# Attention heads in couples: score products alternate between the halves of TensorE's rows, value products between the halves of its columns

## The chip, the cores and the metric

The kernel runs on one core of a Trainium2 chip, in one launch. The metric is the time of an execution on the device in microseconds (us). Three runs of the kernel before took 1774.15, 1775.56 and 1777.96 us. The core's engines work side by side and each takes its own instructions in its own order: TensorE (PE, with PEld for the loads of its weights), VectorE (DVE), ScalarE (ACT), GpSimd (POOL), and SyncE (SP), which here issues the loads of the weights.

## The reference

Two blocks of two layers each on x [1, 256, 1024] in float32; the output of the first is the input of the second. What matters here are the products with only 64 rows or 64 columns:

```
first block, per layer:
  xn = rms_norm(h); proj = xn @ w_in                      # queries, keys, values, gates, RWKV inputs
  y_a: 8 query heads of 64 on 2 key heads, mask = the 64 best causal keys of an indexer
       s = q k^T / 8 ; p = softmax(s + mask) ; o = p v
  y_b: a short convolution, gated
  y_c: RWKV-7, 8 heads of 64: zw = w0 + tanh(lw) @ w_up ; a = sigmoid(a0 + la @ a_up)   # 64 rows each
       a recurrence over the tokens, here in chunks of 64 tokens by products of [64, 128] with [64, 128]
  h += (sum of the gated branches) @ w_out ; h += conv_glu_ffn(rms_norm(h))
second block, per layer:
  a: 16 heads of 64, a mixture of dilated causal patterns, here one softmax with one additive table
  b: 8 differential heads: softmax(q1 k1^T) - lambda softmax(q2 k2^T), each of 64 rows, times v [256, 128]
  h += (sigmoid(ga) (ya @ w_proj_a) + sigmoid(gb) (yb @ w_proj_b)) @ w_out
```

## The kernel before

Features lie on the 128 partitions, tokens along the free dimension. All large products with weights are made three times in float32r, from weights and activations split into a high and a low part (lines 206 to 208 and 244 to 246); ACT makes the high parts (line 184), DVE the low ones (line 185), SP's queue brings the raw weights. All small products are float32, and each such matmul shows in the trace as two passes. I call the products with the weights the stream.

A head of 64 features uses half of the array. Its scores (`softmax`, line 436) are two matmuls at line 445 with 64 rows, on the upper or the lower half of the rows as the head is even or odd: 128 queries by 128 keys, then 128 by 256. DVE adds the mask and takes the extreme (line 447), ACT takes the exponential and the sums (450), DVE the reciprocal (452) and, or ACT in the first block (458), the scaling. `flip_probs` transposes the probabilities in three PE instructions (481) and ACT copies them out (483). `apply` makes the head's output with two matmuls (489 and 490) of 64 columns, written to the upper or lower half of a PSUM bank's partitions. Scores and flips take their banks from the pool `at`, which has two; the outputs take one bank of `pv`.

`pipelined` emits for step i the scores of head i, the probabilities of head i - 1 and the output of head i - 2, with a third of a step between the three. In the second block's part b one step has two softmaxes, of both halves of a differential head. In the first block eight heads make a layer's attention; in the second, two groups of eight heads (part a) and two of four differential heads (part b) make a layer. `rw_prepare` makes the two low-rank products (line 764) one after the other, four matmuls each on one half of the rows. `rw_scores` makes for each of four chunks four matmuls (850) on the upper half of the rows and then four on the lower, each four into one bank of the pool `rk` (two banks). The second block does not use `rk`.

The order of the engines' work comes from two places. `interleave` merges the streams (RWKV, attention and the bulk of projections in the first block; bulk and attention in the second) by estimated times, of which the table `TUNE` gives the factors. Then a scheduling layer below the kernel orders each engine's instructions by readiness, so that a stage's matmuls can be parted by instructions of the stream; the rows under "The change" show what it made of it.

Of the kernel before, what the change touches and what calls it, by code (L numbers as in the profile page):

```python
# [17 lines left out]
S = 256  # L18
# [13 lines left out]
def _const_table():  # L32
    """Tables that depend on the shapes alone, one row per partition."""
# [45 lines left out]
# y <- (x y^2 + RSQRT[0]) y, then with a = x y^2: ((c2 a + c1) a + c0) y  # L79
# [26 lines left out]
def interleave_gen(a, b):  # L106
    """two streams in turn"""
    live = [a, b]
    while live:
        for g in list(live):  # L110
            try:
                yield next(g)
            except StopIteration:
                live.remove(g)


class Core:
# [25 lines left out]
    def slot(self, *shape, dt=F32, name="s", extra=False):  # L143
        """a tile of up to 4 KB per partition from the shared slots, or from those of the present phase"""
# [44 lines left out]
    # ---- activations as matmul operands: pairs of 128-row k tiles (hi, lo), feature on the partition  # L189
# [11 lines left out]
    def block(self, ps, hi, lo, x, ks, nk):  # L201
        """k tiles ks (of nk) of one block of 128 output features [128, 256]"""
# [7 lines left out]
    def feature_pair(self, src, c0, x, nk, pool=None, between=(), ready=None):  # L210
        """two blocks of 128 output features side by side in one bank: [128, 2, 256]; between: calls to make after each"""
# [61 lines left out]
    def rstd(self, ss, n, eps):  # L273
        """(ss / n + eps) ** -0.5 in place"""
# [39 lines left out]
    def squares(self, c, src=None, out=None, ts=(0, 1)):  # L314
        """sums of squares of half c of the columns"""
# [8 lines left out]
    def raw_half(self, g, c, squares=True):  # L324
        """after half c of h is there: its part of the operand without the norm's scale, and of the scale"""
# [16 lines left out]
    def norm_scale(self, eps, ss=None, ts=slice(0, 2)):  # L342
        """the norm's scale of every token [128, 2]"""
# [6 lines left out]
    def rows_of(self, r):  # L350
        """r [128 tokens, 2] along the free dimension of every partition [128, 256]"""
# [10 lines left out]
    def normalise(self, rb, x):  # L362
        """calls that fill the pairs of the operand x of the normalised h"""
# [5 lines left out]
    def last_half(self, w):  # L369
        """after the last layer of the first block: h * the final norm's gains and its squares"""  # L370
# [10 lines left out]
    def row_gains(self, g):  # L381
        """the gains of a norm on every partition"""
# [4 lines left out]
    def flip_pair(self, src, j):  # L387
        """columns 256 j .. of two token tiles, features on the partition: [128, 2, 256] in PSUM"""
# [7 lines left out]
    def residual(self, src, x, nk, after, first=0, between=()):  # L396
        """h += x @ src; after(c) follows half c of the columns"""
# [6 lines left out]
    def finish(self, src, x, nk, g, out):  # L404
        """out = the norm of h + x @ src, with gains g"""
# [17 lines left out]
    # ---- attention pieces  # L423
    def rope(self, q, cc, ss):
        """q [128, heads, d], tables [128, rot]: (x1, x2) -> (x1 cos - x2 sin, x2 cos + x1 sin)"""
# [10 lines left out]
    def softmax(self, qt, kt, mask):  # L436
        """exp(score - max) of one head [128, 384] (tile 0: 128 keys, tile 1: 256) and 1 / sums [128, 2].
        qt holds the negated, scaled queries."""
        nc = self.nc
        ps = self.bank(self.at, 384)  # L440
        e = self.sp.tile([128, 384], F32, tag="e", name="e", bufs=4)
        m = self.sp.tile([128, 2], F32, tag="m", name="m", bufs=4)
        z = self.sp.tile([128, 2], F32, tag="z", name="z", bufs=4)
        for t, (a, n) in enumerate(SPANS):
            nc.tensor.matmul(ps[:, a:a + n], lhsT=qt[:, 128 * t:128 * t + 128], rhs=kt[:, 0:n], start=True, stop=True)  # L445
        for t, (a, n) in enumerate(SPANS):
            nc.vector.tensor_tensor_reduce(out=e[:, a:a + n], in0=ps[:, a:a + n], in1=mask[:, a:a + n], scale=1.0,  # L447
                                           scalar=3e38, op0=ALU.add, op1=ALU.min, accum_out=m[:, t:t + 1])
        for t, (a, n) in enumerate(SPANS):
            nc.scalar.activation(out=e[:, a:a + n], in_=e[:, a:a + n], func=AF.Exp, scale=-1.0, bias=m[:, t:t + 1],  # L450
                                 accum_out=z[:, t:t + 1])
        nc.vector.reciprocal(out=z, in_=z)
        return e, z
# [1016 lines left out]
```

## Time and profile before

| | us |
|---|---|
| median of three runs | 1775.56 |
| span of the profiled execution, from its first to its last instruction | 1782.4 |
| TensorE busy in it | 1742.8 (98%) |
| VectorE busy | 1256.7 (71%) |
| ScalarE busy | 962.4 (54%) |
| mean granted TensorE clock | 0.981 of full speed |

The profiled execution is 6.8 us (0.4%) longer than the median of the runs. Busy time of PE counts modelled ends of pipelined matmuls, so 98% says that PE almost never had nothing to do, not that it ran at its peak. How dense it ran is read from the times at which matmuls start.

### The profile page before, as it was taken

The numbers are of one execution on the slowest core, as the hardware profiler recorded it, in microseconds if no ns is written. First come the engines' busy times: TensorE is split into PE (matmuls) and PEld (weight loads), VectorE is DVE, ScalarE is ACT, GpSimd is POOL, SyncE is SP. The second block draws the span as 40 slices with busy tenths as digits, with TensorE's granted clock in tenths as the row PEclk, the third lists the DMA queues.
The fourth block names the chain that finished last, engine by engine and source line by source line (L and its number), as shares of the span: only waits on it lengthen the run. The fifth ranks groups of instructions, "written<-read, shape, count | busy, mean of one in ns | idle before, by whom it ended". The sixth has DMA issues, their size and how long they took to land.

```text
span 1782.4 us, 30027 instructions
## 1 busy us (share of the span) xinstructions
PE 1742.8 (98%) x12016; PEld 1562.9 (88%) x12016; DVE 1256.7 (71%) x2504; ACT 962.4 (54%) x1688; POOL 72.3 (4%) x81
## 2 busy tenths in 40 slices
PE   8999899999999999999999999999999999999998
PEld 8989789899989988789899887888899878888997
DVE  6589846789957589657789867566666675666666
ACT  6554543556646544534555556556654565556643
POOL 2000201101000000202000000000000000000000
PEclk9999989999999989899999999999999999999999
DMA  7533423565556434224555555344445453444453
GB/s 229 164 107 110 127 71 102 175 197 180 168 192 208 124 117 136 78 70 136 179 188 178 190 183 182 122 137 144 157 147 169 167 188 119 142 143 146 147 175 138
DMA packets 217371, 268.89 MB, mean 151 GB/s; under 512 B 6570, under 2 KB 170716, under 8 KB 217232
## 3 DMA queue, kind: packets, MB, share of 16 engines
q1 hardware_dynamic: 213520, 262.81, 45.4%
q10 hardware_dynamic: 2944, 3.94, 0.7%
q8 instruction: 94, 1.54, 0.4%
q14 instruction: 45, 0.37, 0.1%
q0 software_dynamic: 768, 0.23, 0.1%
HBM read 265.91 MB, written 1.05 MB: 150 GB/s over the span
## 4 chain that ended last, share of the span: by engine, by line
PE 85%; DVE 9%; DMA 3%; ACT 2%; issue 1%; POOL 0%; SPq 0%; ACTq 0%; POOLq 0%
PE ps L206 15%; PE ps L208 15%; PE ps L207 15%; PE ps L246 8%; PE ps L244 8%; PE ps L245 8%; PE ps L445 3%; DVE wlo L185 3%; PE ps L481 2%; PE ps L393 1%; PE ps L489 1%; DMA raw<-in_w_out_dram 1%; ACT whi L184 1%; PE ps L636 1%; DVE pr L893 1%
## 5 line engine op out<-in xcount | busy, mean ns | idle before, releaser
L185 DVE TENSOR_TENSOR wlo<-raw,whi 128x1024 fp32r<-128x1024 f32 (+2 forms) x504 | 617.6, 1228 | 315.4 <-ACT whi L184 304.0
L184 ACT ACTIVATE whi<-raw 128x1024 fp32r<-128x1024 f32 (+2 forms) x504 | 525.5, 1046 | 556.6 <-PE ps L207 287.3
L206 PE MATMUL ps<-op,whi 128*128 128x256 f32 x2464 | 709.5, 288 | 0.1
L208 PE MATMUL ps<-op,wlo 128*128 128x256 f32 x2464 | 703.0, 285 | 2.1 <-DVE wlo L185 2.0
L207 PE MATMUL ps<-op,whi 128*128 128x256 f32 x2464 | 702.2, 285 | 1.2 <-DVE op L199 1.0
L206 PEld LDWEIGHTS ps<-op,whi 128*128 128x128 f32 x2464 | 474.2, 192 | 12.3 <-issue 10.0
L208 PEld LDWEIGHTS ps<-op,wlo 128*128 128x128 f32 x2464 | 474.6, 193 | 6.9 <-issue 3.2
L207 PEld LDWEIGHTS ps<-op,whi 128*128 128x128 f32 x2464 | 474.6, 193 | 5.5 <-issue 3.3
L244 PE MATMUL ps<-whi,op 128*128 128x512 f32 (+2 forms) x784 | 307.1, 392 | 0.8 <-ACT qtok L1188 0.8
L246 PE MATMUL ps<-whi,op 128*128 128x512 f32 (+2 forms) x784 | 303.9, 388 | 1.6 <-DVE op L199 1.6
L245 PE MATMUL ps<-wlo,op 128*128 128x512 f32 (+2 forms) x784 | 303.7, 387 | 1.7 <-DVE wlo L185 1.7
L245 PEld LDWEIGHTS ps<-wlo,op 128*128 128x128 f32 x784 | 149.5, 191 | 31.0 <-DVE wlo L185 3.4
L246 PEld LDWEIGHTS ps<-whi,op 128*128 128x128 f32 x784 | 149.2, 190 | 29.9 <-DVE op L199 2.5
L244 PEld LDWEIGHTS ps<-whi,op 128*128 128x128 f32 x784 | 149.3, 191 | 28.6 <-issue 2.0
L450 ACT ACTIVATE e<-e,m 128x128 f32<-128x128 f32 (+1 forms) x160 | 71.3, 447 | 29.9 <-DVE m L447 29.5
L447 DVE CUSTOM_DVE_ANT_0 e<-ps,consts 128x128 f32<-128x128 f32 (+1 forms) x128 | 41.3, 352 | 34.0 <-PE ps L445 34.0
L445 PE MATMUL ps<-qT 64*128 64x128 f32 (+1 forms) x256 | 46.7, 351 | 1.2 <-DVE m L447 1.2
L199 DVE TENSOR_TENSOR op<-xt,op 128x512 fp32r<-128x512 f32 x48 | 32.2, 688 | 18.8 <-ACT op L198 18.5
L481 PE MATMUL ps<-ident,e 128*128 128x128 f32 x192 | 38.5, 297 | 5.7 <-ACT e L458 3.0
L483 ACT COPY pt<-ps 128x384 f32<-128x384 f32 x64 | 29.9, 472 | 25.3 <-PE ps L481 20.6
L481 PEld LDWEIGHTS ps<-ident,e 128*128 128x128 f32 x192 | 23.0, 146 | 17.8 <-ACT e L458 4.0
L701 DVE SCALAR_TENSOR_TENSOR glu<-ps,vec,glu 128x254 f32<-128x254 f32 x72 | 34.5, 479 | 1.3
(337 smaller groups left out, 1628.3 us busy)
## 6 DMA issues: line engine op xcount, KB each, us to landing
raw<-in_w_in_dram SPq DMA_DIRECT2D x130, 1024.0 KB, 5.2
raw<-in_ffn_up_dram SPq DMA_DIRECT2D x44, 1024.0 KB, 5.1
raw<-in_ffn_down_dram SPq DMA_DIRECT2D x20, 1024.0 KB, 5.1
raw<-in_w_out_dram SPq DMA_DIRECT2D x16, 1024.0 KB, 5.1
raw<-in_w_branch_dram SPq DMA_DIRECT2D x24, 512.0 KB, 3.5
raw<-in_w_proj_a_dram SPq DMA_DIRECT2D x8, 1024.0 KB, 5.2
raw<-in_w_proj_b_dram SPq DMA_DIRECT2D x8, 1024.0 KB, 5.2
raw<-in_w_in_dram SPq DMA_DIRECT2D x8, 768.0 KB, 4.4
```

The costliest lines, as they stand in the source:

```text
L184: nc.scalar.activation(out=hi, in_=v, func=AF.Copy)
L185: nc.vector.tensor_tensor(out=lo, in0=v, in1=hi.bitcast(F32), op=ALU.subtract)
L206: self.nc.tensor.matmul(ps, lhsT=hi[:, k], rhs=xh, start=k == 0, stop=False)
L207: self.nc.tensor.matmul(ps, lhsT=hi[:, k], rhs=xl, start=False, stop=False)
L208: self.nc.tensor.matmul(ps, lhsT=lo[:, k], rhs=xh, start=False, stop=k == nk - 1)
L244: self.nc.tensor.matmul(ps[t][:, :n], lhsT=xh, rhs=hi, start=kk == first, stop=False)
L245: self.nc.tensor.matmul(ps[t][:, :n], lhsT=xh, rhs=lo, start=False, stop=False)
L246: self.nc.tensor.matmul(ps[t][:, :n], lhsT=xl, rhs=hi, start=False, stop=kk == last)
L445: nc.tensor.matmul(ps[:, a:a + n], lhsT=qt[:, 128 * t:128 * t + 128], rhs=kt[:, 0:n], start=True, stop=True)
L447: nc.vector.tensor_tensor_reduce(out=e[:, a:a + n], in0=ps[:, a:a + n], in1=mask[:, a:a + n], scale=1.0, scalar=3e38, op0=ALU.add, op1=ALU ...
L450: nc.scalar.activation(out=e[:, a:a + n], in_=e[:, a:a + n], func=AF.Exp, scale=-1.0, bias=m[:, t:t + 1], accum_out=z[:, t:t + 1])
L481: self.nc.tensor.transpose(ps[:, 128 * j:128 * j + 128], p[:, 128 * j:128 * j + 128], self.ident)
```

## The change

Two heads that use the two halves of the array become one step. `softmax_pair` takes two banks, makes the first matmul of both heads, then the second of both, then both softmaxes with one reciprocal. `apply_pair` alternates the two heads' value products in the same way. In the second block the scores' banks come from `rk`. `pipelined` now emits scores, output, probabilities in a step, over four couples with steps twice as long. `rw_prepare` alternates the two low-rank products, and `rw_scores` the two halves of the rows, with two banks at once. Comments and docstrings are gone too, which moves line numbers: 481 is now 486, 489 and 490 are 496 and 498, 764 is 773, 850 is 861. No matmul is added or removed.

```diff
-    def softmax(self, qt, kt, mask):
...
-        ps = self.bank(self.at, 384)
...
+    def softmax_pair(self, qt, kt, mask, pool):
+        ps = [self.bank(pool, 384) for _ in range(2)]
+        z = self.sp.tile([128, 4], F32, tag="z", name="z", bufs=3)
         for t, (a, n) in enumerate(SPANS):
-            nc.tensor.matmul(ps[:, a:a + n], lhsT=qt[:, 128 * t:128 * t + 128], rhs=kt[:, 0:n], start=True, stop=True)
+            for b in range(2):
+                r = slice(64 * b, 64 * b + 64)
+                nc.tensor.matmul(ps[b][:, a:a + n], lhsT=qt[r, 128 * t:128 * t + 128], rhs=kt[r, 0:n], start=True, stop=True)
+        out = []
+        for b in range(2):
...
         nc.vector.reciprocal(out=z, in_=z)
-        return e, z
+        return out
...
             if i < n:
                 state[i] = heads[i][0]()
                 yield step / 3
+            if 0 <= i - 2 < n:
+                heads[i - 2][2](state.pop(i - 2))
+                yield step / 3
             if 0 <= i - 1 < n:
                 state[i - 1] = heads[i - 1][1](state[i - 1])
                 yield step / 3
-            if 0 <= i - 2 < n:
-                heads[i - 2][2](state.pop(i - 2))
-                yield step / 3
...
-        pt = self.sp.tile([128, 384], F32, tag="pt", name="pt", bufs=2)
+        pt = self.sp.tile([128, 384], F32, tag="pt", name="pt", bufs=3)
...
-    def apply(self, out, pt, v0, v1):
-        nc.tensor.matmul(out, lhsT=v0, rhs=pt[:, 0:256], start=True, stop=False)
-        nc.tensor.matmul(out[:, 128:256], lhsT=v1, rhs=pt[:, 256:384], start=False, stop=True)
+    def apply_pair(self, out, pts, vs):
+        half = lambda b: slice(64 * b, 64 * b + 64)
+        for b in range(2):
+            nc.tensor.matmul(out[half(b)], lhsT=vs[b][0], rhs=pts[b][:, 0:256], start=True, stop=False)
+        for b in range(2):
+            nc.tensor.matmul(out[half(b), 128:256], lhsT=vs[b][1], rhs=pts[b][:, 256:384], start=False, stop=True)
...
-            return lambda: k.softmax(qt[r, 2 * j + a], kt[r, j], mask), probs, out
-        yield from k.pipelined([head(h) for h in range(8)], TUNE["a1"])
+            return lambda: k.softmax_pair(qt[:, i], kt[:, j], mask, k.at), probs, out
+        yield from k.pipelined([pair(i) for i in range(4)], 2 * TUNE["a1"])
...
-        for dst, p0, bias in ((sig, 0, "hw0"), (a, 64, "ha0")):
-            for j in range(2):
-                ps = k.bank(k.rk, 2, S)
+        two = ((sig, 0, "hw0"), (a, 64, "ha0"))
+        for j in range(2):
+            ps = [k.bank(k.rk, 2, S) for _ in two]
+            for i in range(2):
+                b = 2 * j + i
+                for p, (_, p0, _) in zip(ps, two):
+                    nc.tensor.matmul(p[:, i], lhsT=up[p0:p0 + 64, 128 * b:128 * b + 128], rhs=lo[p0:p0 + 64, 0], start=True, stop=True)
...
         for c in range(4):
+            ps = [k.bank(k.rk, 4, 128) for _ in range(2)]
+            for hh in range(4):
+                for p in range(2):
+                    s = slice(64 * p, 64 * p + 64)
+                    nc.tensor.matmul(ps[p][:, hh], lhsT=bk[hh // 2][s, hh % 2, c], rhs=ar[hh // 2][s, hh % 2, c], start=True, stop=True)
...
-                return lambda: k.softmax(qt[r, 2 * j + a], kt[r, 2 * j + a], k.c["dilated"]), probs, out
-            yield from k.pipelined([head(h) for h in range(8)], TUNE["a2"])
+                return lambda: k.softmax_pair(qt[:, i], kt[:, i], k.c["dilated"], k.rk), probs, out
+            yield from k.pipelined([pair(i) for i in range(4)], 2 * TUNE["a2"])
...
-                    return [k.softmax(qt[64 * b:64 * b + 64, i], kt[64 * b:64 * b + 64, i], k.c["causal"]) for b in range(2)]
+                    return k.softmax_pair(qt[:, i], kt[:, i], k.c["causal"], k.rk)
```

On PE, in the second block's first layer, second group of part a, two heads of before stand so (L445 scores, L481 flips, L489 and L490 values, L244 to L246 the stream; numbers are those of buffers):

```order
L481 MATMUL ps_12289<-ident_82,e_12110 128x128 x3
L489 MATMUL ps_12189<-pt_12187,v_11816 64x256
L490 MATMUL ps_12189<-pt_12187,v_11816 64x128
L445 MATMUL ps_12297<-qT_11691,qT_11532 128x128
L445 MATMUL ps_12297<-qT_11691,qT_11532 128x256
L481 MATMUL ps_12310<-ident_82,e_12193 128x128 x3
L489 MATMUL ps_12189<-pt_12293,v_11816 64x256
L490 MATMUL ps_12189<-pt_12293,v_11816 64x128
L244 MATMUL ps_12337<-whi_12341,op_11234 128x512
L445 MATMUL ps_12318<-qT_11691,qT_11532 128x128
L445 MATMUL ps_12318<-qT_11691,qT_11532 128x256
```

The same place of the change, one couple (L486 flips, L496 and L498 values):

```order
L496 MATMUL ps_12276<-pt_12164,v_11812 64x256
L496 MATMUL ps_12276<-pt_12170,v_11812 64x256
L498 MATMUL ps_12276<-pt_12164,v_11812 64x128
L498 MATMUL ps_12276<-pt_12170,v_11812 64x128
L486 MATMUL ps_12285<-ident_82,e_12082 128x128 x3
L486 MATMUL ps_12291<-ident_82,e_12088 128x128 x3
L445 MATMUL ps_12297<-qT_11688,qT_11516 128x128
L445 MATMUL ps_12298<-qT_11688,qT_11516 128x128
L445 MATMUL ps_12297<-qT_11688,qT_11516 128x256
L445 MATMUL ps_12298<-qT_11688,qT_11516 128x256
```

Two separate bursts of values and two of scores have become one of each. In the first block's first layer, PE's first two couples of the change stand so (L206 to L208 the stream):

```order
L445 MATMUL ps_1974<-kT_1970,qT_1949 128x128
L445 MATMUL ps_1975<-kT_1970,qT_1949 128x128
L445 MATMUL ps_1974<-kT_1970,qT_1949 128x256
L445 MATMUL ps_1975<-kT_1970,qT_1949 128x256
L206 MATMUL ps_2368<-op_259,whi_2375 128x256
L207 MATMUL ps_2368<-op_259,whi_2375 128x256
L208 MATMUL ps_2368<-op_259,wlo_2376 128x256
L206 MATMUL ps_2368<-op_259,whi_2375 128x256
L445 MATMUL ps_2038<-kT_1970,qT_1949 128x128
L445 MATMUL ps_2038<-kT_1970,qT_1949 128x256
L445 MATMUL ps_2039<-kT_1970,qT_1949 128x128
L445 MATMUL ps_2039<-kT_1970,qT_1949 128x256
```

The second couple comes four instructions of the stream behind the first, and its heads follow each other instead of alternating. Elsewhere the scheduling layer parts a couple's scores altogether, as here in the first group of part a (second block, first layer):

```order
L445 MATMUL ps_11537<-qT_11327,qT_11217 128x128
L445 MATMUL ps_11537<-qT_11327,qT_11217 128x256
L244 MATMUL ps_11593<-whi_11597,op_11218 128x512
L445 MATMUL ps_11538<-qT_11327,qT_11217 128x128
L445 MATMUL ps_11538<-qT_11327,qT_11217 128x256
```

The scores of the two heads of this couple have an instruction of the stream between them. Counted over PE's whole order: of the 40 couples, both heads' score matmuls stand together in 16 before and in 32 now; of the 24 couples of value products, 8 before and 24 now; places where PE goes over between full-size and smaller tiles, or between kinds of smaller tiles, are 321 before and 270 now (179 and 164 of them in the first block).

## Rows read from the trace of the kernel before

**Rows 1.** The page: span, and busy time of the engines.

```profile
span 1782.4 us, 30027 instructions
...
PE 1742.8 (98%) x12016; PEld 1562.9 (88%) x12016; DVE 1256.7 (71%) x2504; ACT 962.4 (54%) x1688; POOL 72.3 (4%) x81
```

**Rows 2.** The page's chain that ended last, by engine.

```profile
PE 85%; DVE 9%; DMA 3%; ACT 2%; issue 1%; POOL 0%; SPq 0%; ACTq 0%; POOLq 0%
```

**Rows 3.** Windows: stretch, its length, busy us per engine, PEclk, DMA share, GB/s.

```profile
120.00:195.00 75.00, 72.29 (x573) 67.18 (x572) 72.15 (x174) 36.13 (x57) 5.87 (x8) 1.00 0.44 134
195.00:240.00 45.00, 42.49 (x340) 35.25 (x338) 28.02 (x60) 23.35 (x58) 6.87 (x5) 0.77 0.19 60
645.00:720.00 75.00, 70.74 (x534) 64.11 (x532) 69.83 (x169) 34.43 (x57) 5.98 (x7) 0.95 0.39 120
720.00:765.00 45.00, 44.31 (x342) 36.87 (x342) 26.84 (x57) 21.75 (x54) 5.80 (x4) 0.73 0.19 59
1075.00:1350.00 275.00, 273.37 (x1690) 230.99 (x1689) 167.83 (x424) 162.43 (x338) 0.00 (x0) 1.00 0.45 146
```

**Rows 4.** Timeline of PE, one head's scores (start us, us, line, xcount).

```profile
1299.97 0.28 PE L208 MATMUL ps<-op,wlo 128*128 128x256 f32 x1
1300.18 0.92 PE L445 MATMUL ps<-qT 64*128 64x128 f32 x4
1301.03 0.38 PE L206 MATMUL ps<-op,whi 128*128 128x256 f32 x1
1301.25 0.28 PE L207 MATMUL ps<-op,whi 128*128 128x256 f32 x1
1301.37 0.28 PE L208 MATMUL ps<-op,wlo 128*128 128x256 f32 x1
```

**Rows 5.** Timeline of PE, both halves of a differential head.

```profile
1311.41 0.28 PE L208 MATMUL ps<-op,wlo 128*128 128x256 f32 x1
1311.62 0.93 PE L445 MATMUL ps<-qT 64*128 64x128 f32 x8
...
1312.70 0.28 PE L207 MATMUL ps<-op,whi 128*128 128x256 f32 x1
```

**Rows 6.** Timeline of PE, one head's values.

```profile
215.58 0.28 PE L207 MATMUL ps<-op,whi 128*128 128x256 f32 x1
...
216.81 0.28 PE L206 MATMUL ps<-op,whi 128*128 128x256 f32 x1
```

**Rows 7.** Timeline of PE, values of an even and an odd head.

```profile
253.78 0.28 PE L208 MATMUL ps<-op,wlo 128*128 128x256 f32 x1
253.99 0.66 PE L489 MATMUL ps<-pt,av 128*64 128x256 f32 x4
...
255.02 0.28 PE L207 MATMUL ps<-op,whi 128*128 128x256 f32 x1
```

**Rows 8.** Timeline of PE, a burst of `rw_prepare` and one of `rw_scores`.

```profile
70.23 0.28 PE L208 MATMUL ps<-op,wlo 128*128 128x256 f32 x1
70.44 1.99 PE L764 MATMUL ps<-lora,waup 64*128 64x256 f32 x8
...
72.58 0.28 PE L207 MATMUL ps<-op,whi 128*128 128x256 f32 x1
...
156.59 0.28 PE L208 MATMUL ps<-op,wlo 128*128 128x256 f32 x1
156.79 1.71 PE L850 MATMUL ps<-ar,bk 64*128 64x128 f32 x16
...
158.66 0.28 PE L207 MATMUL ps<-op,whi 128*128 128x256 f32 x1
```

**Rows 9.** Waits of PE (waiting, waited for: us in total, times, longest).

```profile
PE ps L481 <- ACT e L458: 3.0, 2, 2.4
...
PE ps L481 <- DVE m L447: 1.8, 6, 0.3
...
PE ps L445 <- DVE m L447: 1.2, 4, 0.3
```

**Rows 10.** Line 452: idle time of DVE before it, until ACT's exponentials.

```profile
L452 DVE RECIPROCAL z<-z x80: 109/160/169, 197.6 to 1687.9; 128x2 f32<-128x2 f32 x80
...
  ACT e L450: 11.7, 21
```

More of the change, by code (lines that the diff above doesn't have):

```diff
@@ L673, in attention, with pair, probs, out @@
         banks = {}
-        def head(h):
-            j, a, b = h // 4, h // 2 % 2, h % 2
-            r = slice(64 * b, 64 * b + 64)
-            def probs(ez):
-                k.scale_rows(*ez, True)
-                return k.flip_probs(ez[0])
-            def out(pt):
-                if h % 4 == 0:
+        def pair(i):
+            j, a = i // 2, i % 2
+            def probs(ezs):
+                for ez in ezs:
+                    k.scale_rows(*ez, True)
+                return [k.flip_probs(e) for e, _ in ezs]
+            def out(pts):
+                if a == 0:
                     banks[j] = k.bank(k.pv, 2, S)
-                k.apply(banks[j][r, a], pt, v[:, 0, 64 * j:64 * j + 64], v[:, 1, 64 * j:64 * j + 64])
-                if h % 4 == 3:
+                k.apply_pair(banks[j][:, a], pts, [(v[:, 0, 64 * j:64 * j + 64], v[:, 1, 64 * j:64 * j + 64])] * 2)
+                if a:
                     k.split(banks[j], *ya[j])
-            return lambda: k.softmax(qt[r, 2 * j + a], kt[r, j], mask), probs, out
-        yield from k.pipelined([head(h) for h in range(8)], TUNE["a1"])
+            return lambda: k.softmax_pair(qt[:, i], kt[:, j], mask, k.at), probs, out
+        yield from k.pipelined([pair(i) for i in range(4)], 2 * TUNE["a1"])
         self.ya = ya
@@ L758, in rw_prepare @@
         sig, a = k.slot(4, S, name="sig"), k.slot(4, S, name="a")
-        for dst, p0, bias in ((sig, 0, "hw0"), (a, 64, "ha0")):
-            for j in range(2):
-                ps = k.bank(k.rk, 2, S)
+        two = ((sig, 0, "hw0"), (a, 64, "ha0"))
[5 more added lines that the diff above has]
+                    nc.tensor.matmul(p[:, i], lhsT=up[p0:p0 + 64, 128 * b:128 * b + 128], rhs=lo[p0:p0 + 64, 0], start=True, stop=True)
+            for p, (dst, _, bias) in zip(ps, two):
                 for i in range(2):
                     b = 2 * j + i
-                    nc.tensor.matmul(ps[:, i], lhsT=up[p0:p0 + 64, 128 * b:128 * b + 128], rhs=lo[p0:p0 + 64, 0], start=True, stop=True)
-                for i in range(2):
-                    b = 2 * j + i
-                    nc.scalar.activation(out=dst[:, b], in_=ps[:, i], func=AF.Tanh, scale=0.5, bias=v[bias][:, b:b + 1])
+                    nc.scalar.activation(out=dst[:, b], in_=p[:, i], func=AF.Tanh, scale=0.5, bias=v[bias][:, b:b + 1])
+            yield 3.0
+        for dst, _, _ in two:
             nc.vector.tensor_scalar(out=flat(dst), in0=flat(dst), scalar1=0.5, scalar2=0.5, op0=ALU.mult, op1=ALU.add)
-            yield 3.0
         self.gt = k.slot(2, 512, name="gtok")
@@ L845, in rw_scores @@
         for c in range(4):
-            for p in range(2):
-                ps = k.bank(k.rk, 4, 128)
-                for hh in range(4):
-                    s = slice(64 * p, 64 * p + 64)
-                    nc.tensor.matmul(ps[:, hh], lhsT=bk[hh // 2][s, hh % 2, c], rhs=ar[hh // 2][s, hh % 2, c], start=True, stop=True)
-                nc.vector.tensor_tensor(out=gm[c][:, 4 * p:4 * p + 4], in0=ps, in1=mask, op=ALU.mult)
+            ps = [k.bank(k.rk, 4, 128) for _ in range(2)]
[3 more added lines that the diff above has]
+                    nc.tensor.matmul(ps[p][:, hh], lhsT=bk[hh // 2][s, hh % 2, c], rhs=ar[hh // 2][s, hh % 2, c], start=True, stop=True)
+            for p in range(2):
+                nc.vector.tensor_tensor(out=gm[c][:, 4 * p:4 * p + 4], in0=ps[p], in1=mask, op=ALU.mult)
             yield 2.5
@@ L1331, in attend, with pair, probs, out @@
             banks = {}
[L1333 to L1335 removed]
+            def pair(i):
+                j, a = i // 2, i % 2
                 jj = 2 * half + j
[L1338 to L1343 removed]
+                def probs(ezs):
+                    for ez in ezs:
+                        k.scale_rows(*ez)
+                    return [k.flip_probs(e) for e, _ in ezs]
+                def out(pts):
+                    if a == 0:
                         banks[j] = k.bank(k.pv, 2, S)
[L1345 to L1346 removed]
+                    k.apply_pair(banks[j][:, a], pts, [[v[:, t, 64 * h:64 * h + 64] for t in range(2)] for h in (2 * i, 2 * i + 1)])
+                    if a:
                         self.pre["a", jj] = y = k.temp(2, S, name="ypre")
                         nc.scalar.copy(y, banks[j])
[L1350 to L1352 removed]
+                return lambda: k.softmax_pair(qt[:, i], kt[:, i], k.c["dilated"], k.rk), probs, out
+            yield from k.pipelined([pair(i) for i in range(4)], 2 * TUNE["a2"])
             for jj in (2 * half, 2 * half + 1):
```

28 lines of the change are left out of this document (9 added, 19 removed).

## The prediction

> **What bounds the kernel now.** I read the busy times first, then the chain that ended last, then windows over the stages that the change touches, and last the start times of single matmuls. The busy times put PE at 98% of the span of 1782.4 us, DVE at 71%, ACT at 54% [rows 1]; 85% of the chain that ended last is PE [rows 2]. So what shortens PE's own work shortens the kernel, unless another engine is full in that stage. The windows tell where that is so [rows 3]. In the attention of the second block (1075 to 1350 us, and a second stretch like it in the last layer) PE is busy for 273.37 of 275 us and DVE for 167.83, ACT for 162.43: PE alone is the bound. In the first block, while RWKV's triangular solve runs on DVE (120 to 195 us and 645 to 720 us), DVE is busy for 72.15 and 69.83 of 75 us: there PE and DVE are both nearly full. Behind these, at 195 to 240 and 720 to 765 us, the granted clock is 0.77 and 0.73 on average: the two levels are 1.2 and 2.4 GHz, so 0.46 and 0.54 of 45 us, 21 and 24 us, ran at the lower one.
>
> **Whether two halves run at once.** Start to start, an instruction of the stream takes 0.12 us: 1301.25 to 1301.37 [rows 4]. One head's scores (four passes) take 1301.25 - 1299.97 = 1.28 us from the instruction of the stream ahead of them to the second one behind; less two places of the stream that is 1.04 us on top of it [rows 4]. The two halves of a differential head, eight passes, take 1312.70 - 1311.41 = 1.29 us, so 1.05 us on top [rows 5]. The second half is free, although before gives all matmuls of the first half and then all of the second. For the columns the same: one head's values cost 216.81 - 215.58 = 1.23 us, 0.99 on top [rows 6]; two heads that stand together cost 255.02 - 253.78 = 1.24, 1.00 on top [rows 7]. So this core does run the two halves side by side, and before already does it wherever two heads happen to stand together. The change is worth what it adds to that.
>
> The Trainium skill, "TensorE: Matmul & The Clock Gate", section Part 3, says that matmuls start and end strictly in program order. By that rule the differential heads would have run one half after the other before, and alternating them would gain 16 couples more. The trace disagrees: eight passes take the time of four [rows 4, 5]. By the rule the sum below would be larger by 16 x 0.64 = 10.2 us and the time 1737 us; it gets a chance of 0.01.
>
> **Prices.** A burst of small tiles has passes and two changes of the tile size, in and out. `rw_prepare`'s burst, eight passes of 256 columns on one half, takes 72.58 - 70.23 = 2.35, 2.11 on top [rows 8]. A head's scores are two passes of 128 and two of 256 columns; if time goes with columns that is three of 256, at 1.04. From 8p + c = 2.11 and 3p + c = 1.04: p = 0.214 us for a pass of 256 columns, 0.107 for 128, and c = 0.40 us for the two changes, 0.20 each. A head's scores are then 0.64 us of passes, its values 0.99 - 0.40 = 0.59 us.
>
> **The sum on PE.** The counts are those of the order, under "The change".
> - Scores: 32 couples stand together instead of 16. 16 x 0.64 = 10.2 us less.
> - Values: 24 instead of 8. 16 x 0.59 = 9.4 us less.
> - Changes of tile size: 321 - 270 = 51 fewer, 51 x 0.20 = 10.2 us less.
> - `rw_prepare`: four bursts of eight passes of which four now run beside the other four: 4 x 4 x 0.214 = 3.4 us less.
> - `rw_scores`: six whole bursts (three chunks per layer; the first chunk waits piece by piece for its operands before and after). A burst takes 158.66 - 156.59 = 2.07, 1.83 on top, 1.43 without the changes [rows 8]; 16 passes one by one would be 1.71, so the two halves already overlap in part. At best 8 x 0.107 = 0.86: 6 x 0.57 = 3.4 us less.
>
> Together 36.6 us. Against that, six of the 32 couples stand close behind another step's, head after head: two per layer in the first block (one is shown under "The change") and one per layer in the second block's part b. Their second head needs a bank that DVE empties only then, so I count these as serial: 6 x 0.64 = 3.8 us. That leaves 32.8 us, of which the second block has 20.7 (ten of the couples' scores, 6.4, twelve of values, 7.1, and 142 - 106 = 36 changes, 7.2) and the first block 12.1 (four couples of values, 2.4, 15 changes, 3.0, and `rw_prepare` and `rw_scores`; its scores gain nothing, since its four new couples are the serial ones).
>
> How much of it arrives: in the second block all, since PE is the bound and DMA is at 0.45 of its share [rows 3]. In the first block `rw_scores` and part of the attention lie in or just behind the stretch in which DVE is nearly full; what PE saves there it partly waits for. Bounds are nothing lost (0) and all lost (12.1); I take a third, 4 us, since only `rw_scores`' 3.4 us lie wholly within that stretch. 32.8 - 4 = 28.8 us.
>
> **The rest of the change.** A couple has one reciprocal instead of two, 40 fewer of 0.16 us on DVE, 6.4 us; DVE waited 11.7 us for the exponentials in front of them, now for four of them at once, so this wait may halve or double (-6 to +12 us) [rows 10]. DVE has 107 us free in the 275 of each attention stretch of the second block, which hides both. PE waited 3.0 + 1.8 + 1.2 = 6.0 us for softmax's engines and banks [rows 9]; the new banks in `rk` let the second block's flips keep `at` to themselves, and the probabilities come later after the scores, so up to these 6 us may go; as many may come in the first block, where scores now take both banks of `at`. I count zero, with 6 us to either side. What waits behind a PE instruction that waits for a bank is the whole stream. Output before probabilities: the flips come a third of a step later, the copies on ACT have as long as before. Nothing on SP's queue or POOL's is moved. The clock: I count no change.
>
> So 1782.4 - 28.8 = 1753.6 for a profiled execution. The profiled one of before is 6.8 us above the median; taken off the median, 1775.6 - 28.8 = 1746.8. I predict 1747 us; the likeliest case's own range is 1740 to 1753, from the waits of 6 us to either side.
>
> **Rivals.**
> - First block gains nothing. DVE is nearly full for 75 us per layer [rows 3], scores there take both banks of `at` at once, and their second couple stands right behind the first; PE then waits for DVE what it saved. For it: those rows, and the wait of 2.4 us for a scaled exponential [rows 9]. Against: PE is fully busy for most of the block. Then only the second block's 20.7 us are gained: 1755 us. The Trainium skill, "TensorEngine Tiling (Array Packing)", section Restrictions and Gotchas, speaks for it: row tiling raises the pressure on PSUM, since different row tiles write to different banks. The order agrees in that eight of the 40 couples stay parted.
> - The clock recovers. 21 + 24 us at 1.2 GHz behind the solve cost up to half, 22 us [rows 3]. Heads as couples shorten the small products there; if half of the low stretches goes, 11 us more are gained: 1736 us. Against: the smallest products there are RWKV's, which the change does not touch.
> - Slower: alternation itself makes the halves serial. No row of before shows matmuls that alternate; rows 5 and 7 show two runs, one per half. If PE must finish one half before it turns to the other, the 16 couples of scores and the eight of values that run together now lose 10.2 + 4.7 us, and `rw_scores` 6 x 0.28 = 1.7, against 10.2 us of fewer changes: 6 us slower, 1782 us, and with 0.20 us at each turn (three per couple, 64 couples: 38 us) 1820. It decides from the point where eight alternating passes take over 1.7 us. Against: eight passes of both halves show as one stretch of 0.93 us where four take 0.92 [rows 4, 5], so the array works on both at once and takes up the second half before the first is through.
>
> **Chances.** Forecast 0.57, first block gains nothing 0.22, clock recovers 0.11, the rule of strict order 0.01, slower 0.05; 0.04 for what I have not thought of, most of it near no change. The range of 1731 to 1761 holds the first three cases with 5 to 6 us at each end for the waits, and leaves out under 2 in 10. A run of this kernel can be told from no change from about 0.2%, 3.6 us. Faster by more: 0.92; within: 0.03; slower: 0.05.
>
> **What would show it.** Eight passes of scores in about 0.9 us at 26 to 32 places, eight of values in about 0.8 us at 24; a burst of `rw_prepare` with 2.11 - 0.86 = 1.25 us on top of the stream and one of `rw_scores` with 1.83 - 0.57 = 1.26; the stretch of the second block's attention shorter by about 10 us per layer, PE as full as before. The first rival shows as idle PE in the first block, on scores or flips behind DVE, with its mixing stage no shorter. The second shows in the granted clock. Two heads' passes with starts 0.1 us apart or more instead of nearly together would make the prediction wrong.

## The result, and the profile after

The kernel after takes 1743.16 us (median of four runs, 1742.73 to 1745.99) beside 1776.24 us of the kernel before; the ratio is 0.9821 with an interval of 0.9807 to 0.9835. The time forecast was 1747 us.

The page of the kernel after: span, busy times and the chain that ended last, to be set beside [rows 1, 2].

```profile
span 1740.9 us, 30007 instructions
...
PE 1700.2 (98%) x12016; PEld 1539.7 (88%) x12016; DVE 1250.7 (72%) x2464; ACT 957.2 (55%) x1688; POOL 72.4 (4%) x81
...
PE 81%; DVE 11%; DMA 4%; ACT 3%; issue 2%; POOL 0%; ACTq 0%; SPq 0%; POOLq 0%; DVEq 0%
```

PE has the same 12016 instructions and 42.6 us less to do, and the span lost 41.5. The engine that was full is as full as before, and what came off it came off the span.

Where it went: one instruction of the stream in the first block's last stage (the 5,401st of 9,744 in both kernels) and the last one of the stream, in the timeline of before and then of after.

```profile
944.27 0.28 PE L206 MATMUL ps<-op,whi 128*128 128x256 f32 x1
...
1773.75 0.39 PE L246 MATMUL ps<-whi,op 128*128 128x512 f32 x1
```

```profile
927.56 0.28 PE L206 MATMUL ps<-op,whi 128*128 128x256 f32 x1
...
1732.31 0.39 PE L246 MATMUL ps<-whi,op 128*128 128x512 f32 x1
```

From the one to the other it is 829.5 us before and 804.8 after: the second block gains 24.7 us, and none of it is the clock's, since the granted clock is 1.00 all the way between the two rows in both. Up to the first row 16.7 us are gained, but not all by the change. The windows of after over the stages of [rows 3]:

```profile
120.00:195.00 75.00, 71.26 (x555) 65.52 (x554) 71.43 (x179) 37.14 (x64) 9.70 (x11) 0.98 0.40 123
195.00:240.00 45.00, 42.12 (x389) 36.28 (x388) 27.28 (x48) 24.68 (x59) 2.55 (x2) 0.85 0.19 60
640.00:715.00 75.00, 68.93 (x544) 62.73 (x542) 72.07 (x183) 37.41 (x70) 11.35 (x9) 0.98 0.43 134
715.00:765.00 50.00, 48.77 (x451) 44.01 (x452) 28.87 (x56) 24.90 (x54) 0.00 (x0) 0.83 0.14 44
1060.00:1330.00 270.00, 269.23 (x1755) 232.94 (x1755) 172.51 (x428) 163.49 (x342) 0.00 (x0) 1.00 0.47 153
```

In the second block PE is busy for 269.23 of 270 us, as full as in [rows 3], with 1755 instead of 1690 of PE's records in less time. In the first block PE is idle for 3.7 and 6.1 us of the two stretches in which DVE is full (2.7 and 4.3 before). Behind them the granted clock is 0.85 and 0.83, so 2 x 0.15 x 45 = 13.5 and 2 x 0.17 x 50 = 17 us at 1.2 GHz, where before had 21 and 24.

That difference of clock belongs to these two executions and not to the kernels. Each run lists its span and its mean granted clock; over 35 runs of the kernel before the clock was 0.981 to 0.989, and the longer spans had the lower clock (correlation -0.88). I multiply each run's span by its clock: what it would be at the full clock, an estimate that takes every stretch at the lower clock to be PE's. Over those 35 runs this has a standard deviation of 1.6 us where the times have 2.8, and it is used below beside the medians. The clock is listed in steps of 0.001, which is 1.8 us of a run, so differences of about 1 us between means of four runs tell nothing. Before: mean clock 0.9857, 1747.2 us at the full clock. After: 0.9855, 1716.6. The change is worth 30.6 us, and the mean clock is the same.

The same bursts as in [rows 5, 7 and 8], in the timeline of PE (start us, us, line, count): a couple's scores, a couple's values, `rw_prepare`, `rw_scores`.

```profile
1143.56 0.28 PE L208 MATMUL ps<-op,wlo 128*128 128x256 f32 x1
1143.77 0.93 PE L445 MATMUL ps<-qT 64*128 64x128 f32 x8
...
1144.85 0.28 PE L207 MATMUL ps<-op,whi 128*128 128x256 f32 x1
...
246.87 0.28 PE L208 MATMUL ps<-op,wlo 128*128 128x256 f32 x1
247.08 0.65 PE L496 MATMUL ps<-pt,av 128*64 128x256 f32 x4
247.56 0.39 PE L498 MATMUL ps<-pt,av 128*64 128x128 f32 x4
...
248.10 0.28 PE L207 MATMUL ps<-op,whi 128*128 128x256 f32 x1
...
70.25 0.28 PE L208 MATMUL ps<-op,wlo 128*128 128x256 f32 x1
70.45 1.13 PE L773 MATMUL ps<-lora,waup 64*128 64x256 f32 x8
...
71.74 0.28 PE L207 MATMUL ps<-op,whi 128*128 128x256 f32 x1
...
145.22 0.28 PE L208 MATMUL ps<-op,wlo 128*128 128x256 f32 x1
145.43 1.16 PE L861 MATMUL ps<-ar,bk 64*128 64x128 f32 x16
...
146.74 0.28 PE L207 MATMUL ps<-op,whi 128*128 128x256 f32 x1
```

From the stream's instruction ahead to the second one behind, less two places of 0.12 us: 1.05 us for the scores of two heads (one head: 1.04), 0.99 for the values (one head: 0.99), 1.25 for `rw_prepare` (2.11 before), 1.28 for `rw_scores` (1.83 before). 24 couples of values stand together; so do 26 of scores, while six run head after head, four in the first block and two in the second.

### The profile page after: what moved, and what is told of

It reads as the page before. It is cut to its first block, busy times and chain, and to the rows that moved or that the text cites. A ratio compares the mean times of both kernels' runs of the same rounds, so it can differ in the third digit from the quotient of the medians.

```text
span 1740.9 us, 30007 instructions
## 1 busy us (share of the span) xinstructions
PE 1700.2 (98%) x12016; PEld 1539.7 (88%) x12016; DVE 1250.7 (72%) x2464; ACT 957.2 (55%) x1688; POOL 72.4 (4%) x81
## 3 DMA queue, kind: packets, MB, share of 16 engines
HBM read 265.91 MB, written 1.05 MB: 153 GB/s over the span
## 4 chain that ended last, share of the span: by engine, by line
PE 81%; DVE 11%; DMA 4%; ACT 3%; issue 2%; POOL 0%; ACTq 0%; SPq 0%; POOLq 0%; DVEq 0%
PE ps L206 15%; PE ps L207 15%; PE ps L208 15%; PE ps L246 8%; PE ps L244 8%; PE ps L245 8%; DVE wlo L185 4%; PE ps L445 2%; PE ps L393 2%; DMA raw<-in_ffn_down_dram 1%; DMA raw<-in_w_in_dram 1%; ACT whi L184 1%; PE ps L486 1%; DVE pr L905 1%; PE ps L949 1%
## 5 line engine op out<-in xcount | busy, mean ns | idle before, releaser
L206 PE MATMUL ps<-op,whi 128*128 128x256 f32 x2464 | 710.6, 288 | 0.1
L208 PE MATMUL ps<-op,wlo 128*128 128x256 f32 x2464 | 702.2, 285 | 1.3 <-DVE wlo L185 1.2
L206 PEld LDWEIGHTS ps<-op,whi 128*128 128x128 f32 x2464 | 474.8, 193 | 11.2 <-issue 8.5
L208 PEld LDWEIGHTS ps<-op,wlo 128*128 128x128 f32 x2464 | 474.9, 193 | 3.8 <-DVE wlo L185 1.8
L244 PE MATMUL ps<-whi,op 128*128 128x512 f32 (+2 forms) x784 | 306.2, 391 | 0.8 <-ACT qtok L1200 0.8
L246 PE MATMUL ps<-whi,op 128*128 128x512 f32 (+2 forms) x784 | 303.2, 387 | 1.3 <-DVE op L199 1.3
L246 PEld LDWEIGHTS ps<-whi,op 128*128 128x128 f32 x784 | 148.5, 189 | 30.0 <-DVE op L199 2.2
L244 PEld LDWEIGHTS ps<-whi,op 128*128 128x128 f32 x784 | 148.6, 190 | 29.4 <-issue 2.0
L445 PE MATMUL ps<-qT 64*128 64x256 f32 (+1 forms) x256 | 35.8, 351 | 1.0 <-DVE m L451 0.8
L488 ACT COPY pt<-ps 128x384 f32<-128x384 f32 x64 | 28.8, 480 | 12.9 <-PE ps L486 7.6
L1039 POOL TENSOR_TENSOR gate<-gate,up 128x512 f32<-128x512 f32 x16 | 26.0, 1627 | 212.3 <-DVE up L1038 169.6
L708 DVE SCALAR_TENSOR_TENSOR glu<-ps,vec,glu 128x255 f32<-128x255 f32 x72 | 34.3, 476 | 0.2
```

What stands on the lines that cost most here:

```text
L206: self.nc.tensor.matmul(ps, lhsT=hi[:, k], rhs=xh, start=k == 0, stop=False)
L208: self.nc.tensor.matmul(ps, lhsT=lo[:, k], rhs=xh, start=False, stop=k == nk - 1)
L244: self.nc.tensor.matmul(ps[t][:, :n], lhsT=xh, rhs=hi, start=kk == first, stop=False)
L246: self.nc.tensor.matmul(ps[t][:, :n], lhsT=xl, rhs=hi, start=False, stop=kk == last)
L445: nc.tensor.matmul(ps[b][:, a:a + n], lhsT=qt[r, 128 * t:128 * t + 128], rhs=kt[r, 0:n], start=True, stop=True)
```

## Experiments

All twelve stood beside runs of the kernel before on the same chip. "Full clock" is the mean of span times clock, less the 1747.2 us of the kernel before.

| kernel | median us | ratio to before (95%) | mean clock | full clock, to before |
|---|---|---|---|---|
| after | 1743.16 | 0.9821 (0.9807 to 0.9835) | 0.9855 | -30.6 |
| second block only | 1753.48 | 0.9871 (0.9850 to 0.9892) | 0.9838 | -25.1 |
| first block only | 1767.93 | 0.9956 (0.9939 to 0.9972) | 0.9862 | -5.6 |
| grouped | 1745.48 | 0.9830 (0.9812 to 0.9849) | 0.9858 | -28.7 |
| same half of the rows | 1761.05 | 0.9919 (0.9901 to 0.9937) | 0.9840 | -16.1 |
| RWKV's two edits only | 1773.76 | 1.0008 (0.9995 to 1.0022) | 0.9843 | -2.2 |
| two pools | 1737.71 | 0.9797 (0.9784 to 0.9811) | 0.9850 | -37.2 |
| same half of the columns | 1752.66 | 0.9875 (0.9858 to 0.9892) | 0.9882 | -16.3 |
| two pools, both kinds near | 1739.45 | 0.9806 (0.9792 to 0.9820) | 0.9835 | -38.2 |
| banks of `at` | 1743.74 | 0.9820 (0.9800 to 0.9841) | 0.9858 | -30.2 |
| old order of stages | 1740.83 | 0.9803 (0.9782 to 0.9823) | 0.9862 | -32.4 |
| two pools, near in part a | 1734.24 | 0.9772 (0.9750 to 0.9794) | 0.9854 | -39.2 |
| RWKV's products twice | 1754.18 | 0.9879 (0.9859 to 0.9899) | 0.9840 | -23.1 |

**Which block.** Two kernels have the change in one block and the old code in the other.

> The second block's attention as in the kernel after, the first block's attention, rw_prepare and rw_scores as before. Theory (each block gains what its own products save on PE, as the profiles' landmarks have it: 24.7 us in the second block, 8 of the median's 33 us in the first): 1776.2 - 24.7 = 1751.5 us, between 1749 and 1755. Rival (the second block gains only the 20.7 us of the sum and the first block more than I counted, 12): 1755.5 us. Rival (the gain of the second block comes only with the first block's clock and shifts): 1760 us or more.

> The first block as in the kernel after, the second block's attention as before. Theory: 1776.2 - 8 = 1768 us, between 1765 and 1771, with the first block's cold stretches (1.2 GHz) shorter than before. Rival (the first block gains nothing, PE waits for DVE what it saved): 1776 us. Rival (PE saves 12 us there and loses none of them): 1764 us.

Measured: 1753.48 and 1767.93 us. The second is the theory's case. The first lies midway between the theory's 1751.5 and the rival's 1755.5; at the full clock 25.1 and 5.6 us are gained, which is the theory's 24.7 and not the rival's 20.7, and in the profile, between the two instructions named above, the second block takes 803.7 us in the first kernel (804.8 after) and 829.2 in the second (829.5 before). Together 30.7 us, as much as the whole change. The blocks add up and the second carries four fifths. The rival by which the first block gains nothing is out.

**Alternating, or only standing together.**

```diff
-        for t, (a, n) in enumerate(SPANS):
-            for b in range(2):
+        for b in range(2):
+            for t, (a, n) in enumerate(SPANS):
```

(the loops of `apply_pair`, `rw_prepare` and `rw_scores` likewise)

> The kernel after, but no two matmuls alternate: all of one half, then all of the other, in the scores, the values, rw_prepare and rw_scores; couples still stand together. Theory (standing together is enough: PE takes up the second half while the first still runs): a couple's scores and values take what they take in the kernel after, only rw_scores (16 passes) loses about 0.55 us in each of four bursts: 1743.2 + 2 = 1745 us, at most 1749. Rival (the alternation carries the gain, matmuls run in program order): 26 couples of scores x 0.64, 24 of values x 0.59, rw_prepare 3.4 and rw_scores 3.4 are lost, 37.6 us: 1781 us. In between, if only the first passes of the second half overlap: 1755 to 1770 us.

Measured: 1745.48 us, 1.9 us more than after at the full clock. A couple's scores and one burst of `rw_scores` in that kernel:

```profile
1145.37 0.28 PE L208 MATMUL ps<-op,wlo 128*128 128x256 f32 x1
1145.58 0.93 PE L445 MATMUL ps<-qT 64*128 64x128 f32 x8
...
1146.66 0.28 PE L207 MATMUL ps<-op,whi 128*128 128x256 f32 x1
...
146.61 0.28 PE L208 MATMUL ps<-op,wlo 128*128 128x256 f32 x1
146.82 1.71 PE L860 MATMUL ps<-ar,bk 64*128 64x128 f32 x16
...
148.69 0.28 PE L207 MATMUL ps<-op,whi 128*128 128x256 f32 x1
```

and a burst of `rw_prepare`, four passes of 256 columns on each half:

```profile
70.51 0.28 PE L208 MATMUL ps<-op,wlo 128*128 128x256 f32 x1
70.72 1.14 PE L772 MATMUL ps<-lora,waup 64*128 64x256 f32 x8
...
72.02 0.28 PE L207 MATMUL ps<-op,whi 128*128 128x256 f32 x1
```

The couple takes 1.29 us, the same as alternated; `rw_prepare` takes 1.51, nearly the 1.49 of after; `rw_scores` takes 2.08 instead of 1.52, about as before. With four passes on a half, order does not matter; with eight it does. That the time met the theory's 1745 is in part luck: the edit also moved some couples in PE's order (30 of the 40 stand together, 32 in after), and in the profile the second block, which has no `rw_scores`, takes 806.1 us instead of 804.8. What the slower bursts of `rw_scores` cost in time is not shown.

**The halves themselves.** Matmuls of the same shapes, but both heads on one half, so that the outputs are other ones: of the rows for the scores, of the columns for the values.

```diff
-                r = slice(64 * b, 64 * b + 64)
+                r = slice(0, 64)
```

(for the values, `apply_pair` writes both heads to one half, one head after the other; in the grouped kernel that order by itself costs nothing, 1.00 us on top where alternated values take 0.99)

> The kernel after, but both heads of a couple take their scores from the lower half of the rows (the even head's products are made twice, the odd head's not at all). Same matmuls, same banks, same order; only the two halves of the rows cannot work at the same time. Theory (a couple's scores are free when both halves run): 26 couples that run side by side x 0.64 = 16.7 us: 1743.2 + 16.7 = 1760 us. Rival (the gain is in fewer changes of tile size, in banks and in the other engines, not in the halves): 1743 us.

> The kernel after, but the values' products of both heads of a couple go to the same half of the columns (head by head; the even and odd couple of a bank take the lower and the upper half, so the outputs of heads stand at other places and the result is another). Same matmuls, shapes and banks. Theory (a couple's second values are free because the two halves of the columns run at once): 24 x 0.59 = 14.2 us lost: 1757 us. Rival (values gain only from standing together): 1743 to 1745 us.

Measured: 1761.05 and 1752.66 us; at the full clock 14.5 and 14.3 us more than after. By the median the second looks smaller (9.5), since its runs had the highest clock of all, 0.9882. A couple's scores in the first:

```profile
1152.50 0.28 PE L208 MATMUL ps<-op,wlo 128*128 128x256 f32 x1
1152.71 1.57 PE L445 MATMUL ps<-qT 64*128 64x128 f32 x8
...
1154.44 0.28 PE L207 MATMUL ps<-op,whi 128*128 128x256 f32 x1
```

and a couple's values in the second:

```profile
248.38 0.28 PE L208 MATMUL ps<-op,wlo 128*128 128x256 f32 x1
248.59 0.65 PE L496 MATMUL ps<-pt,av 128*64 128x256 f32 x2
...
250.26 0.28 PE L207 MATMUL ps<-op,whi 128*128 128x256 f32 x1
```

1.94 where the two halves take 1.29, and 1.88 where they take 1.23: the second head costs 0.65 us in both, and that is what the other half of the array hides (the prices were 0.64 and 0.59).

**RWKV's two edits by themselves, and doubled.** First the kernel before with the new loops of `rw_prepare` and `rw_scores` alone; then the kernel after with each of these products made twice.

```diff
-            for hh in range(4):
+            for hh in (0, 1, 2, 3) * 2:
```

(the loop of `rw_prepare` likewise)

> The kernel before with rw_prepare and rw_scores of the kernel after alone. Theory (PE is the bound there too): four bursts of rw_prepare at 1.50 instead of 2.35 us, 3.4, and four whole bursts of rw_scores at 1.52 instead of 2.07, 2.2: 1775.5 - 5.6 = 1770 us. Rival (these bursts lie beside DVE's full stretch, PE waits for what it saved): 1775 us.

> The kernel after, but every alternating product of rw_prepare and rw_scores is made twice into the same place (same result): per layer 2 x 8 passes of 256 columns and 4 x 16 of 128 more, side by side 0.86 us each, 3.4 + 6.9 = 10.3 us more of PE's time in the first block. Theory (in this stretch DVE sets the pace, and PE gives back there whatever it saves or spends, as the kernel with these two edits alone suggests, which came out the same as before): 1743 to 1746 us, and PE's wait for the masked products of rw_scores shrinks. Rival (PE is the bound there and the gain of these two edits is in the kernel after): 1743.2 + 10.3 = 1753 us.

The first came out as its rival: no change in the runs, 2.2 us gained at the full clock, where its bursts should save PE 5.6. Its windows, to be set beside the first and third of [rows 3]:

```profile
120.00:195.00 75.00, 68.92 (x551) 63.48 (x550) 72.40 (x174) 36.35 (x60) 9.91 (x11) 1.00 0.40 129
645.00:720.00 75.00, 67.12 (x520) 61.10 (x519) 69.44 (x170) 35.31 (x64) 13.00 (x9) 0.95 0.39 127
```

and the wait of PE that heads its list and is not among the longest of before:

```profile
PE ps L867 <- DVE gm L855: 4.0, 2, 3.3
```

PE has 3.4 and 3.6 us more of idle time in the stretches where DVE is full, and waits for DVE's masking of the very products that it made sooner. But the rival's reason fits `rw_scores` alone. `rw_prepare`'s bursts lie ahead of those stretches, in the first layer from 70 us on, where DVE is busy for 42.86 of 60 us in the kernel before:

```profile
60.00:120.00 60.00, 58.09 (x397) 53.16 (x396) 42.86 (x105) 33.84 (x55) 0.00 (x0) 0.94 0.41 126
```

Which of the two edits' savings was lost, this run does not tell. And the second kernel contradicts the theory drawn from the first, that PE's time is free there: some 10.3 us added (an estimate from the prices) cost 11.0 by the medians and 7.5 at the full clock, and PE's wait for the masked products, which should have shrunk, is 3.7 us (2.7 in after). So of 5.6 us taken from PE 2.2 arrived, and of 10.3 added 7.5. That both engines are near the bound in the full stretches, so that a gain on one is held up by the other and a loss is not, would explain it; no run shows it. What these two edits are worth within the whole change was not run.

**Why the second block gained more than the sum.**

```diff
-                return lambda: k.softmax_pair(qt[:, i], kt[:, i], k.c["dilated"], k.rk), probs, out
+                return lambda: k.softmax_pair(qt[:, i], kt[:, i], k.c["dilated"], k.at), probs, out
```

(part b likewise; the other kernel has the two lower stages of `pipelined` in the old order)

> The kernel after, but the second block's scores take their banks from the pool at, as the flips do and as before; rk stays unused there. What it tells: in the second block's attention of the kernel before a step's flips that stood alone took 0.52 us on top of the stream, in the kernel after 0.25, twelve and ten times; that and like waits are the some 4 us that the second block gained beyond my sum. Theory (the flips waited for banks that scores held): they wait again, 1743.2 + 3.7 = 1747 us, and the flips' bursts are near 0.5 again. Rival (the flips waited for the probabilities, and the steps twice as long mended it): 1743 us, flips at 0.25.

> The kernel after, but a step emits scores, probabilities, output as before, not scores, output, probabilities. Theory (the order of the stages is worth nothing, the number of changes of tile size is 170 in both): 1743 us, between 1741 and 1745. Rival (flips right behind the scores wait for the scaled probabilities; ten to twelve flips lose 0.27 us each): 1746 us.

A flip of before that waits, with the stream around it (the release in brackets):

```profile
1312.70 0.28 PE L207 MATMUL ps<-op,whi 128*128 128x256 f32 x1
1313.28 0.55 PE L481 MATMUL ps<-ident,e 128*128 128x128 f32 x3 [0.29 <-DVE m L447]
...
1313.78 0.28 PE L206 MATMUL ps<-op,whi 128*128 128x256 f32 x1
```

and one of after that does not:

```profile
1304.58 0.28 PE L208 MATMUL ps<-op,wlo 128*128 128x256 f32 x1
1304.70 0.49 PE L486 MATMUL ps<-ident,e 128*128 128x128 f32 x3
...
1305.15 0.28 PE L207 MATMUL ps<-op,whi 128*128 128x256 f32 x1
```

The first is 0.84 us on top of the stream, the second 0.33, which is three passes. Taken over the second block, of the flips that stand alone before, six cost 0.84 us and six 0.33; after, all ten cost 0.33. That is 6 x 0.51 = 3.1 us. The six waited for a bank of `at` that scores held until DVE had read it [rows 9]. With the new order and the old pool all ten cost 0.33 again, with the old order and the new pool eight cost 0.32 to 0.40, and neither kernel is slower than after by more than the noise (at the full clock 0.4 us slower and 1.8 faster). So either of the two edits removes this wait, and neither is needed beside the other. The theory that gave it to the pool (1747 us) missed, and so did the rival that gave it to the order (1746). That the order by itself is worth nothing came out, except that the old order is rather the better one: 1740.83 us lies just below the range given, and in its profile the second block takes 803.1 us (804.3 with the old pool, 804.8 after).

**Further along the same way.** In after some couples still wait for the banks of the couple before, and scores and values stand in bursts of their own.

```diff
-                return lambda: k.softmax_pair(qt[:, i], kt[:, i], k.c["dilated"], k.rk), probs, out
+                return lambda: k.softmax_pair(qt[:, i], kt[:, i], k.c["dilated"], (k.rk, k.at)[i % 2]), probs, out
```

(part b likewise; the second and third kernel also leave out the third of a step between a couple's scores and the values of the couple two steps before, "near" in the table: the second in both blocks, the third in the second block's part a)

> The kernel after, but in the second block the scores of every second couple take their banks from the pool at instead of rk, so that the second couple of a group need not wait for the first one's banks. In the order 14 bursts of scores stand directly behind another burst, and seven couples that were parted stand whole. Theory (a change of tile size costs 0.20 us, a parted couple 0.64): 28 x 0.20 + 7 x 0.64 = 10 us: 1743.2 - 10 = 1733 us. Rival (the flips, which use at alone in the kernel after, now wait for those banks): 1743 us or more.

> The kernel after with two things more: the two pools of scores' banks in the second block, and, for the heads with 64 values, a couple's scores and the values of the couple two steps before stand in one burst (no third of a step between them). In the order the number of changes of tile size among these products falls from 170 to 130, and nine couples that were parted stand whole. Theory: 40 x 0.20 + 9 x 0.64 = 13.8 us: 1743.2 - 13.8 = 1729 us. Rival (a change from the rows' halves to the columns' halves costs as much as both changes through the full array, so ten places are no gain): 1733 us. Rival (waits for banks and for the copies eat it): 1740 us or more.

> The kernel after with the two pools of scores' banks in the second block, and there, for the heads of part a, a couple's scores and the values of two steps before in one burst; the first block as in the kernel after. Theory (the second block gains 8 us more than in the kernel after, as in the profile of the version that had this in both blocks, and the first block's cold stretches stay as short as in the kernel after): 1743.2 - 8 = 1735 us. Rival (the burst of both kinds gains nothing over the two pools alone): 1738 us. Rival (the longer cold stretches of that version came with this): 1740 us.

Measured: 1737.71, 1739.45 and 1734.24 us. All three beat the kernel after, by 6.6, 7.6 and 8.6 us at the full clock. Two couples of scores in one burst, in the first of them:

```profile
1267.60 0.28 PE L208 MATMUL ps<-op,wlo 128*128 128x256 f32 x1
1267.81 1.58 PE L445 MATMUL ps<-qT 64*128 64x128 f32 x16
...
1269.55 0.28 PE L207 MATMUL ps<-op,whi 128*128 128x256 f32 x1
```

1.95 us, so 1.71 on top where two bursts take 2 x 1.05: the missing 0.39 us are two changes of the tile size. But the first two kernels gained two thirds and half of the 10 and 13.8 us that I expected; the third met its 8. Twice in the second block three couples now stand in one burst, and that takes 4.17 us where three couples' passes, two changes and two places of the stream (0.23 us each there, with 512 columns) are 3 x 0.64 + 0.40 + 0.46 = 2.78: PE is idle twice in it, for 0.33 and 0.27 us, before matmuls of the third couple, which waits for banks. What the burst of scores and values adds over the two pools is not settled: the second block takes 797.3 us in the profile of the two pools alone (804.8 after), 796.8 with the burst in both blocks and 797.1 with it in the second. 1734.24 us is the best time; its lead over 1737.71 is not shown to come from the edit.

## Why the prediction was right

- **Two halves run at once already; alternating adds nothing to a couple that stands together.** Right: 1.29 us alternated and grouped. The rule of strict order, which gave 1737 us by another way, is out: it would have put the grouped kernel at 1781.
- **Prices.** 0.64 and 0.59 us for a second head: 0.65 and 0.65. 0.40 for two changes of the tile size: 0.39. The bursts of `rw_prepare` and `rw_scores`: 1.25 and 1.28 on top where 1.25 and 1.26 stood in the sum.
- **Second block, 20.7 us.** 24.7 in the profiles, 25.1 in the runs at the full clock. The term that was too small is the waits, counted at zero with 6 us to either side: the flips' wait for banks went, about 3 of the 4 us. The rest of the difference is open.
- **First block, 12.1 us less 4.** 5.6 at the full clock instead of 8.1. The term that was mis-sized is the loss: counted as a third, 4 us, it was 6.5 of 12.1. One part is known: whole bursts of `rw_scores` that gained were four and not six, 2.2 us instead of 3.4, since in each layer a second chunk waits for its operands. `rw_prepare` and `rw_scores` alone bring 2.2 us, so if the parts add up, which was not run, 3.4 are the attention's, where the sum had 5.4. That the loss lies in the stretches in which DVE is full, as I put it, is likely for `rw_scores` and not shown for the rest.
- **Six serial couples.** There were six, four in the first block and two in the second; one of the latter takes 1.97 us where a whole couple takes 1.29.
- **The clock, counted at no change.** Right on the mean of the runs (0.9857 and 0.9855). The rival of the recovered clock would have been read out of the two profiles alone (0.981 and 0.986); more runs say that it is chance.
- **The reciprocal, at zero.** DVE waits 8.8 us for the exponentials in front of it, 11.7 before [rows 10], and DVE has free time in the second block. No run tested it.
- **The rivals.** The first block does gain. Alternation does not make the halves serial: 1.05 us on top for eight passes, far from the 1.7 from which it would decide.

Too small by some 4 us in one block and too large by 2.5 in the other, the sum of 28.8 us came near 30.6 partly because the two errors cancel: that much is luck. Of the 4 us by which 1743.16 lies below the forecast, these two make some 2; another 1 is the base, 1775.6 us from three runs, where 35 later ones have a median of 1774.3.

## What to carry to other kernels

Where products use half of the array, put two that use different halves next to each other in the order of the engine, in banks that are both free: here that alone made the second one free, and whether their matmuls alternate mattered for eight passes on a half and not for four. Price each burst as its passes plus the two changes of tile size at its ends, and count bursts before and after, not instructions. In a stretch where two engines are both nearly full, do not count in full what you take from one of them; what you add cost most of its price here.

## What the runs showed of the hardware

- Sixteen passes of 128 columns, eight on each half: 1.28 us on top when they alternate, 1.84 when one half's eight stand before the other's. Without the two changes (0.40) and with 0.107 us a pass, that is eight passes' time and 13 to 14. The single starts of the second agree: 13 steps, the first four and the last five of one pass each, and in three of the four between them two passes start 3 to 6 ns apart. With four passes on a half, one half before the other, every step has two, 13 to 14 ns apart. So passes of the second half start while the first half's are still to come, but in the long burst only three of eight find a partner. I read this as a look-ahead of a few passes; how far it reaches was not measured.
- The same program's mean granted clock moved between 0.981 and 0.989 from run to run, which is some 14 us of its span; span times clock was steadier than the time, and it told apart what the medians blurred (same half of the columns, RWKV's edits alone).
